# Feed-forward gates and ups by seven half-block products instead of eight, with their result kept in DRAM

## The chip, the cores and the metric

The kernel runs on one core of a Trainium2 chip. The metric is the device time of one execution in microseconds (us), the median over several runs. The engines are named as in the profile: PE is TensorE (PEld its weight load), DVE is VectorE, ACT is ScalarE, POOL is GpSimd, SP is the engine whose queue issues the DMAs.

## What is computed

A trunk of two layers. Each layer normalises the residual stream, puts it through one input projection, three kinds of token mixers and an output projection, and then through a SwiGLU feed-forward; both results are added with a gate. Scale, shift and gate are "modulation" columns, computed from `c` and `c_ctx` by a product with `mod_w`. The change is in the feed-forward (512 latent tokens and, in layer 0 only, 256 context tokens; width 1024; 2816 hidden units):

```python
def swiglu(h, w_in, w_out):
    gate, up = jnp.split(h @ w_in, 2, axis=-1)
    return (jax.nn.silu(gate) * up) @ w_out
...
    for i in range(DEPTH):
        ctx_out = i < DEPTH - 1
        ...
        xl = xl + gt1_l * (jnp.concatenate([ya_l, yb_l, ym_l], axis=-1) @ w_out[i])
        xl = xl + gt2_l * swiglu(modulate(rmsnorm(xl, norm2_g[i]), sh2_l, sc2_l), ffn_w_in[i], ffn_w_out[i])
        if ctx_out:
            xc = xc + gt1_c * (jnp.concatenate([ya_c, yb_c, ym_c], axis=-1) @ w_out[i])
            xc = xc + gt2_c * swiglu(modulate(rmsnorm(xc, norm2_g[i]), sh2_c, sc2_c), ffn_w_in[i], ffn_w_out[i])
```

## The kernel before, in words

Everything is float32. A float32 product is made of three matmuls in the type fp32r: each operand is split into a rounded part (`hi`, a copy by ScalarE, line 227) and the rest (`lo`, a subtraction by VectorE or GpSimd, line 228), and hi x hi, hi x lo and lo x hi are summed in PSUM. `weight` loads 128 output columns of a matrix with a DMA on SP's queue into `wr` and splits them into `wh` and `wl` (two buffers each). `gemm` runs over the 128-row pages of the contraction and makes the three matmuls of each page (line 262) for each span of tokens: 512 columns, and in layer 0 another 256. The result stands in one of five PSUM buffers `gm`.

The last part of a layer goes like this. The mixers' result is split into pages; for each of eight output tiles m of 128 rows `residual` (line 1323) adds the output projection, times its modulation, to X in SBUF. The norm (`norm_stat`, `norm_scale`, `norm_page`) makes the pages `hpage` of the feed-forward's input: a multiply that reads X and a PSUM row of scales (line 364), a scale and shift by ScalarE (line 365), and a split, the odd pages' by GpSimd. The 22 hidden tiles of 128 units are then done in three parts of 8, 7 and 7 (`PARTS`). For each tile of a part the gate and up columns are loaded, multiplied with the eight pages, and joined: ScalarE's tanh (line 1490) and two VectorE rows (lines 1491 and 1492) make silu(gate) x up, which is split into a page `hid` that stays in SBUF. After each part, for each m, the matching rows of the second matrix are multiplied with these pages and added to X.

The modulation columns that later parts of the kernel need are made on VectorE between all this, by `mod_some`: it takes some of a list `todo`, loads a page `wd` of 512 KB and reduces it against `silu(c)` (`mod_dve`, line 320). In layer 0's feed-forward it takes two after each hidden tile and one after each m.

Nothing orders these steps by hand but `issue_after` and `behind`, which keep an instruction behind another: a scheduler puts each engine's instructions in a fixed order when the kernel is built, and pools with a given number of buffers decide how far one step can run ahead of another. Each engine goes through its own list in order, and SP through its DMAs.

Of the kernel before, what the change touches and what calls it, by code (L numbers as in the profile page):

```python
# [11 lines left out]
F32 = mybir.dt.float32  # L12
# [3 lines left out]
ALU = mybir.AluOpType  # L16
# [28 lines left out]
PARTS = (8, 7, 7)  # L45
EPS = 1e-6
# [130 lines left out]
def trunk(ctx, tc, I, out, dbg=None):  # L177
# [194 lines left out]
    xs = dr.tile([P, KD, TL], F32, name="xs")  # L372

# [969 lines left out]

    early = ExitStack()
    xm = early.enter_context(pool("xm"))
    with pool("x0") as xp, pool("p0", 2, space=PSUM) as pm:
# [4 lines left out]
        cb, t = silu_rows(xm, pm)  # L1351
# [26 lines left out]
    marks = (md, mm)  # L1378
    todo = [(0, m) for m in range(16, 48)] + [(1, m) for m in range(48)]

    def mod_some(n, wk, bufs, ins):

        with tc.issue_after(ins.ins):
            for _ in range(min(n, len(todo))):
                mod_dve(*todo.pop(0), cb, t, wk, bufs)

    for l in range(DEPTH):
# [6 lines left out]
        with pool(f"pm{l}", 2, space=PSUM) as pm, pool(f"pc{l}", 1, space=PSUM) as pc, \  # L1394
# [7 lines left out]
            with pool(f"tp{l}") as tp, behind(marks if l == 0 else ()):  # L1402
                data = rwkv_in(l, ctx_out, h, rp, rq, tp, pm, pgm, both, lambda i: mod_some(2 if l == 0 else 0, xm, 4, i))
# [23 lines left out]
        with ExitStack() as st:  # L1427
            xp = st.enter_context(pool(f"x{l + 1}", 1, "right"))
            X = xp.tile([P, KD, T], F32, name="X")
            with behind(loads[3:4]):  # L1430
                xload(X, l)
            tmp = st.enter_context(pool(f"ft{l}", 2, "right"))
            pm = st.enter_context(pool(f"ps{l}", 2, space=PSUM))
            pgm = st.enter_context(pool(f"pf{l}", 5, space=PSUM))
            if l == 0:
                cb, t = silu_rows(tmp, pm)

            yh = pages(KD, KORD)
# [91 lines left out]
```

## Time and profile before

| | |
|---|---|
| median of 3 runs | 2280.55 us (2273.83 to 2282.71) |
| the profiled execution: its time, its span | 2283.55 us, 2281.8 us |
| TensorE busy, granted clock | 95%, .959 |
| VectorE, ScalarE, GpSimd busy | 61%, 37%, 14% |
| share of the chain that ended last | TensorE 81%, VectorE 10%, ScalarE 4% |
| `gm` matmuls of line 262 in that chain | 57% |

The profile is of one execution. Busy shares are averages over the whole span; the chain follows the work that ended last backwards, so it says where each engine set the end. A matmul's time is best read from the distance of its start from the next one's, since matmuls overlap in the pipeline.

### The profile page before, as it was taken

What the parts mean: (1) busy time and instruction counts of PE and PEld (TensorE: products, weight loads), DVE (VectorE), ACT (ScalarE), POOL (GpSimd) and SP (SyncE); (2) the same over time, 40 slices, a digit from 0 to 9 for tenths busy, and PEclk for the clock granted to TensorE, in tenths of its full rate; (3) what the DMA queues carried; (4) which work ended last, traced back from release to release, by engine and by line L of the source; (5) the groups of instructions that cost most, each with busy time, mean ns of one, the idle gap of its engine ahead of it and who ended that gap; (6) DMA issues with size and microseconds to landing.
All of it is one profiled execution on the core that took longest, in us unless ns stands there. A gap on an engine that the chain in (4) does not pass through costs nothing.

```text
span 2281.8 us, 36365 instructions
## 1 busy us (share of the span) xinstructions
PE 2159.2 (95%) x14604; PEld 1780.9 (78%) x14604; DVE 1381.9 (61%) x2706; ACT 844.7 (37%) x1527; POOL 314.2 (14%) x482
## 2 busy tenths in 40 slices
PE   7999997997999999999999999999898998999999
PEld 4788886784668788888888878787685677888887
DVE  6687777895547766554444455788796545334343
ACT  4433333664552421122122354433473544222231
POOL 1022322332201100000000111113142211000000
PEclk9999997897999999999999989999697998999999
DMA  7241112232115334344432312211232122323323
GB/s 289 84 153 52 62 41 74 77 88 56 42 70 155 100 114 146 111 129 135 133 112 83 109 52 63 73 57 39 85 100 59 35 74 83 101 94 94 100 92 102
DMA packets 87352, 211.99 MB, mean 93 GB/s; under 512 B 10248, under 2 KB 33680, under 8 KB 86544
## 3 DMA queue, kind: packets, MB, share of 16 engines
q1 hardware_dynamic: 87184, 209.67, 29.2%
q8 instruction: 115, 1.88, 0.3%
q14 instruction: 53, 0.43, 0.1%
HBM read 187.62 MB, written 22.02 MB: 92 GB/s over the span
## 4 chain that ended last, share of the span: by engine, by line
PE 81%; DVE 10%; ACT 4%; DMA 2%; issue 2%; POOL 1%; SPq 0%; DVEq 0%; ACTq 0%; POOLq 0%
PE gm L262 57%; PE po L1034 4%; PE psm L585 2%; PE inv L660 2%; PE st L1028 1%; DVE cT L320 1%; PE st L1029 1%; PE st L1030 1%; PE mx L1008 1%; PE psm L514 1%; PE pB L700 1%; DVE wl L228 1%; PE psm L573 1%; ACT hu L365 1%; PE up L246 1%
## 5 line engine op out<-in xcount | busy, mean ns | idle before, releaser
L262 PE MATMUL gm<-hpage,wh 128*128 128x512 f32 (+1 forms) x3744 | 1001.7, 355 | 15.3 <-ACT hpage L227 8.9
L262 PEld LDWEIGHTS gm<-hpage,wh 128*128 128x128 f32 x3744 | 664.2, 191 | 119.8 <-ACT hpage L227 11.0
L262 PE MATMUL gm<-hpage,wl 128*128 128x512 f32 (+1 forms) x1872 | 657.4, 353 | 1.9 <-DVE wl L228 1.8
L227 ACT ACTIVATE wh<-wr 128x1024 fp32r<-128x1024 f32 (+2 forms) x214 | 221.6, 1036 | 560.7 <-PE gm L262 457.6
L262 PEld LDWEIGHTS gm<-hpage,wl 128*128 128x128 f32 x1872 | 358.1, 191 | 50.6 <-DVE wl L228 2.5
L228 DVE TENSOR_TENSOR wl<-wr,wh 128x1024 fp32r<-128x1024 f32 (+2 forms) x214 | 258.2, 1207 | 186.9 <-ACT wh L227 185.1
L262 PE MATMUL gm<-hid,wh 128*128 128x512 f32 (+1 forms) x1056 | 282.6, 356 | 0.0
L262 PEld LDWEIGHTS gm<-hid,wh 128*128 128x128 f32 x1056 | 185.6, 188 | 32.2
L262 PE MATMUL gm<-hid,wl 128*128 128x512 f32 (+1 forms) x528 | 187.4, 356 | 0.0
L1323 DVE SCALAR_TENSOR_TENSOR X<-gm,mod,X 128x512 f32<-128x512 f32 (+1 forms) x100 | 64.0, 643 | 191.0 <-PE gm L262 187.7
L320 DVE CUSTOM_DVE_ANT_0 cT<-wd,cB,mod_b 128x1024 f32<-128x1024 f32 x140 | 177.7, 1300 | 1.1 <-DMA wd<-in_mod_d 0.7
L1492 DVE SCALAR_TENSOR_TENSOR ft<-ft,gm 128x512 f32<-128x512 f32 x66 | 39.5, 598 | 153.0 <-PE gm L262 152.7
L1010 DVE TENSOR_REDUCE mr<-mx 128x1 fp32r<-128x768 f32 (+1 forms) x80 | 67.9, 848 | 83.8 <-PE mx L1008 83.6
L1034 PE MATMUL po<-pe,hpage 128*128 128x512 f32 (+1 forms) x224 | 112.2, 590 | 0.5 <-ACT pe L1032 0.4
L262 PEld LDWEIGHTS gm<-hid,wl 128*128 128x128 f32 x528 | 99.0, 188 | 16.1
L338 POOL TENSOR_TENSOR acc<-acc,sq 128x512 f32<-128x512 f32 (+1 forms) x15 | 23.9, 1601 | 604.0 <-ACT sq L337 604.0
L1032 ACT ACTIVATE pe<-st 128x512 f32<-128x512 f32 (+1 forms) x112 | 62.9, 563 | 89.8 <-PE st L1030 88.7
L227 ACT ACTIVATE hid<-ft 128x512 fp32r<-128x512 f32 x66 | 36.2, 549 | 128.4 <-DVE ft L1492 128.4
L1028 PE MATMUL st<-k,k 97*128 97x512 f32 (+1 forms) x112 | 78.0, 698 | 4.7 <-ACT k L1015 4.1
L1490 ACT ACTIVATE ft<-gm 128x512 f32<-128x512 f32 x66 | 33.9, 514 | 90.4 <-PE gm L262 90.3
L1008 PE MATMUL mx<-k,k 96*128 96x256 f32 (+1 forms) x144 | 46.3, 396 | 17.1 <-DVE mr L1010 9.9
L585 PE MATMUL psm<-pr,kb 64*128 64x128 f32 (+1 forms) x384 | 57.7, 308 | 1.4 <-POOL pr L555 1.4
(425 smaller groups left out, 3128.5 us busy)
## 6 DMA issues: line engine op xcount, KB each, us to landing
wr<-in_ffn_in SPq DMA_DIRECT2D x88, 512.0 KB, 3.5
wd<-in_mod_d SPq DMA_DIRECT2D x86, 512.0 KB, 3.8
wr<-in_w_in SPq DMA_DIRECT2D x44, 512.0 KB, 3.6
wr<-in_ffn_out SPq DMA_DIRECT2D x34, 448.0 KB, 3.4
wr<-in_w_out SPq DMA_DIRECT2D x20, 512.0 KB, 3.7
wr<-in_ffn_out SPq DMA_DIRECT2D x16, 512.0 KB, 3.6
zs<-ze SPq DMA_DIRECT2D x26, 256.0 KB, 2.0
X<-in_xT SPq DMA_DIRECT2D x16, 384.0 KB, 6.4
```

Source lines behind the costliest of these rows:

```text
L227: ac.activation(hi, src, AF.Copy)
L228: return en.tensor_tensor(lo, src, hi.bitcast(F32), ALU.subtract)
L262: pe.matmul(ps, x[:, j], act[k][y][:, a:b], start=(i == 0 and n == 0), stop=(i == len(kl) - 1 and n == 2))
L320: ve.tensor_tensor_reduce(out=t[:, s], in0=w, in1=cb[:, s], scale=1.0, scalar=modb[:, l, m:m + 1], op0=ALU.mult, op1=ALU.add, accum_out=mo ...
L585: pe.matmul(pa[j][:, p, c], flat(kb[hr, d, p, c]), flat(pr[hr, d, p, c, 0:nq]), start=True, stop=True)
L660: i = pe.matmul(v8(o)[hr, q], a[hr, d, p, c], b[hr, d, p, c], start=True, stop=True)
L1008: pe.matmul(ps[:, a - k0:b - k0], qh[0:96, n * P:(n + 1) * P], kh[0:96, a:b], start=True, stop=True)
L1010: ve.tensor_reduce(mr[:, n - q0:n - q0 + 1], ps[:, :T - k0], AX.X, ALU.max)
L1028: pe.matmul(ps, kh[0:97, ks], qh[0:97, qs], start=True, stop=False)
L1032: ac.activation(e, ps, AF.Exp, scale=QK_SCALE)
L1034: pe.matmul(po[:, :w], v, e, start=(kt == kts[0]), stop=(kt == kts[-1]))
L1323: return ve.scalar_tensor_tensor(X[:, m, a:b], ps, mods[l][:, 24 * which + 16 + m, s:s + 1], X[:, m, a:b], ALU.mult, ALU.add)
```

## The change

A pair of gate and up columns of one hidden tile, 256 output columns in all, against 1024 rows and all tokens, is seen as a 2 by 2 block product: the blocks of the weights are gate and up by upper and lower four pages, those of the activations are upper and lower four pages by first and second half of the tokens. Of the 22 tiles of each layer the first two (`PLAIN`) are done as before; for the other 20 the eight block products are replaced by seven products of sums of blocks (Strassen's scheme in Winograd's form).

- The sums of activation blocks are made once for each layer (`halves`: eight subtractions by VectorE, eight by GpSimd, twelve splits, and four more splits before the first such tile). For that the norm keeps its unsplit output in `ru`, all eight pages.
- The sums of weight blocks are made for each tile: four additions of 128x512 by GpSimd (`wsum`, lines 1472 to 1475 of the new kernel) and five splits of 128x512 (`ws`), beside the split of the gate columns.
- The seven products of a tile have 4 pages x 3 matmuls each on half of the tokens (`product`); seven additions on VectorE, each reading one PSUM buffer, and ScalarE's copy of the first product put them together, then the tanh and three VectorE rows make `hid`.
- All 22 tiles are now done before the second matrix. `hid` (unsplit) is written to DRAM (`hd`) and fetched page by page (`fetch`), then split again (`resplit`). X is also written to DRAM (`xm`) and loaded again for the second matrix.
- The modulation reduces move: in layer 0 none stands among the gates; 2 after each m of the output projection as before, and about 72 reduces in the second matrix's three parts (`mod_some(1)` ahead and 1, 3, 2 behind each m); a last part of them in layer 1. `silu_rows`, 16 small transposes, is made anew for the second matrix of each layer.

```diff
+    def halves(l, nt, ru, h, tq):
+
+        n = nt // 2
+        r = []
+        for k in range(4):
+            b11, b12, b21, b22 = ru[:, k, :n], ru[:, k, n:nt], ru[:, k + 4, :n], ru[:, k + 4, n:nt]
...
+            ve.tensor_tensor(b11, b12, b11, ALU.subtract)
+            gp.tensor_tensor(t3, b22, b12, ALU.subtract)
+            ve.tensor_tensor(b22, b22, b11, ALU.subtract)
+            gp.tensor_tensor(b21, b21, b22, ALU.subtract)
+            for t, src in ((t1, b11), (t2, b22), (t4, b21)):
+                split(t[:, 0], t[:, 1], src)
...
+            if j < PLAIN:
...
+            else:
+                if j == PLAIN:
+                    for k in range(4):
+                        b12 = tuple(x[:, n:nt] for x in h[k])
+                        split(*b12, ts[k][2])
...
+                    B = {1: half(0, lo), 2: half(4, lo), 3: half(4, up), 4: tt(3), 5: tt(0), 6: tt(1), 7: half(0, up)}
+                gh, gl, g = weight(I["ffn_in"][l, j, 0], KD, P, raw=True)
+                u = ws.tile([P, KD, P], F32, name="wu", bufs=2)
+                sp.dma_start(out=u, in_=I["ffn_in"][l, j, 1])
+                s1, s2, s3, s4 = (ws.tile([P, 4, P], F32, name="wsum", bufs=3) for _ in range(4))
+                gp.tensor_tensor(s1, u[:, 0:4], u[:, 4:8], ALU.add)
+                gp.tensor_tensor(s2, s1, g[:, 0:4], ALU.subtract)
+                gp.tensor_tensor(s3, g[:, 0:4], u[:, 0:4], ALU.subtract)
+                gp.tensor_tensor(s4, g[:, 4:8], s2, ALU.subtract)
+                A = {1: (gh[:, 0:4], gl[:, 0:4]), 2: (gh[:, 4:8], gl[:, 4:8])}
+                for i, src in ((6, s2), (7, s3), (5, s1), (4, u[:, 4:8]), (3, s4)):
+                    t = ws.tile([P, 2, 4, P], F32R, name="ws", bufs=7)
+                    split(t[:, 0], t[:, 1], src)
+                    A[i] = (t[:, 0], t[:, 1])
+
+                def product(i):
+                    ps = pgm.tile([P, 512], F32, name="gm")[:, :n]
+                    for k in range(4):
+                        for x, y in ((0, 0), (0, 1), (1, 0)):
+                            pe.matmul(ps, A[i][x][:, k], B[i][k][y], start=(k == 0 and x + y == 0),
+                                      stop=(k == 3 and x == 1))
+                    return ps
...
+                ac.activation(c1, product(1), AF.Copy)
+                ve.tensor_tensor(c2, c1, product(6), ALU.add)
+                ve.tensor_tensor(c1, c1, product(2), ALU.add)
+                ac.activation(t1, c1, AF.Tanh, scale=0.5)
+                ve.scalar_tensor_tensor(t1, t1, 1.0, c1, ALU.add, ALU.mult)
+                ve.tensor_tensor(c3, c2, product(7), ALU.add)
+                p5 = product(5)
+                ve.tensor_tensor(ups[:, n:nt], c3, p5, ALU.add)
+                ve.tensor_tensor(c2, c2, p5, ALU.add)
+                ve.tensor_tensor(ups[:, 0:n], c3, product(4), ALU.add)
+                ve.tensor_tensor(g2, c2, product(3), ALU.add)
+                ac.activation(t2, g2, AF.Tanh, scale=0.5)
+                ve.scalar_tensor_tensor(t2, t2, 1.0, g2, ALU.add, ALU.mult)
+                ve.scalar_tensor_tensor(hid[:, :nt], hid[:, :nt], 0.5, ups[:, :nt], ALU.mult, ALU.mult)
+            sp.dma_start(out=hd[l][j, :, :nt], in_=hid[:, :nt])
...
+            def before(m):
+                if part == 0:
+                    mod_some(1)
+
+            def done(m, ins):
+                more(1)
...
+                elif l == 0:
+                    mod_some((1, 3, 2)[part], ins)
...
+    def fetch(l, j, nt, pool, name):
+
+        t = pool.tile([P, 2, T], F32R, name=name)
+        sp.dma_start(out=t[:, 1, :nt].bitcast(F32), in_=hd[l][j, :, :nt])
+        resplit(t[:, :, :nt])
+        return t[:, 0], t[:, 1]
```

The order of the instructions on three places, before and after. Line numbers move a little: the split's subtraction is line 228 before and 229 after, the norm's multiply 364 and 365.

VectorE among the gates of layer 1, before: one hidden tile with its two weight splits (`wl`) and its silu (numbers tell tiles of one name apart).

```order
L228 TENSOR_TENSOR wl_18470<-wr_18468,wh_18469 128x1024
L1491 SCALAR_TENSOR_TENSOR ft_18462<-ft_18462,gm_18412 128x512
L1492 SCALAR_TENSOR_TENSOR ft_18462<-ft_18462,gm_18437 128x512
L228 TENSOR_TENSOR wl_18476<-wr_18474,wh_18475 128x1024
L228 TENSOR_TENSOR hid_18411<-ft_18462,hid_18411 128x512
```

VectorE at the same place after: one of the 20 tiles. `c` and `ups` with a `gm` among their inputs are the additions that read a product in PSUM; `ws` and `wl` are splits, of this tile's weights and of those of tiles to come; `hid` the silu.

```order
L229 TENSOR_TENSOR wl_20696<-wr_20694,wh_20695 128x1024
L1498 TENSOR_TENSOR c3_20443<-c2_20442,gm_20490 128x256
L1497 SCALAR_TENSOR_TENSOR hid_20409<-hid_20409,c1_20441 128x256
L229 TENSOR_TENSOR ws_20577<-wu_20558,ws_20577 128x512
L1500 TENSOR_TENSOR ups_20445<-c3_20443,gm_20504 128x256
L1501 TENSOR_TENSOR c2_20442<-c2_20442,gm_20504 128x256
L229 TENSOR_TENSOR ws_20580<-wsum_20563,ws_20580 128x512
L1502 TENSOR_TENSOR ups_20445<-c3_20443,gm_20519 128x256
L229 TENSOR_TENSOR ws_20710<-wsum_20703,ws_20710 128x512
L1503 TENSOR_TENSOR c4_20444<-c2_20442,gm_20533 128x256
L1505 SCALAR_TENSOR_TENSOR hid_20409<-hid_20409,c4_20444 128x256
L1506 SCALAR_TENSOR_TENSOR hid_20409<-hid_20409,ups_20445 128x512
```

A tile has nine rows whose inputs both lie in SBUF (`ws`, `wl`, `hid`), and seven that read PSUM stand between them, never more than two in a row.

GpSimd at the start of layer 1's feed-forward and to its end, before: the mixers' last rows, the norm's sums and page splits.

```order
L765 TENSOR_TENSOR ph<-vt,bs 128x2x2x64
L995 MEMSET k_17660 1x768
L994 TENSOR_TENSOR k_17661<-kq,k_17660 96x768
L338 TENSOR_TENSOR acc<-acc,sq 128x512 x3
L228 TENSOR_TENSOR hpage<-hu,hpage 128x256 x8
```

GpSimd there after: the last of `halves`, then the weight sums.

```order
L1399 TENSOR_TENSOR ru<-ru 128x256 x3
L1472 TENSOR_TENSOR wsum<-wu 128x512
L1473 TENSOR_TENSOR wsum<-wsum,wr 128x512
L1474 TENSOR_TENSOR wsum<-wr,wu 128x512
L1475 TENSOR_TENSOR wsum<-wr,wsum 128x512
```

Before, GpSimd has no row among the gates; now four for each of the 20 tiles follow each other to the end of its list, and nothing else stands between.

VectorE in the norm of layer 0 between output projection and feed-forward, before: `hu` is a page times its scale, `hpage` a page's split.

```order
L364 TENSOR_TENSOR hu<-X,psm 128x512 x3
L228 TENSOR_TENSOR wl<-wr,wh 128x1024
L338 TENSOR_TENSOR acc<-acc,sq 128x256
L228 TENSOR_TENSOR hpage<-hu,hpage 128x512
L364 TENSOR_TENSOR hu<-X,psm 128x512
L228 TENSOR_TENSOR hpage<-hu,hpage 128x512
```

VectorE there after: the product now goes to `ru`.

```order
L1326 SCALAR_TENSOR_TENSOR X<-gm,mod_85,X 128x256
L365 TENSOR_TENSOR ru<-X,psm 128x512 x8
L339 TENSOR_TENSOR acc<-acc,sq 128x256
L229 TENSOR_TENSOR wl<-wr,wh 128x1024
L229 TENSOR_TENSOR hpage<-ru,hpage 128x512 x2
L350 TENSOR_SCALAR ms<-ss 128x2
```

Before, three pages are multiplied ahead of the first split, and the other five between splits; now all eight come first.

## Rows read from the trace of the kernel before

**Rows 1.** Part 1 of the page: busy time and share of the span.

```profile
PE 2159.2 (95%) x14604; PEld 1780.9 (78%) x14604; DVE 1381.9 (61%) x2706; ACT 844.7 (37%) x1527; POOL 314.2 (14%) x482
```

**Rows 2.** The chain, in order of time: start, length, engine, line, count (us).

```profile
771.38 530.00 PE gm L262 x3027
...
1912.23 365.77 PE gm L262 x1584
```

**Rows 3.** Stretches: length, busy us and count of PE, PEld, DVE, ACT, POOL; clock, DMA.

```profile
772.00:1302.00 530.00, 530.00 (x3034) 465.78 (x3033) 272.19 (x407) 112.64 (x164) 7.88 (x6) 1.00 0.38 120
794.07:810.75 16.68, 16.68 (x99) 14.77 (x98) 10.34 (x17) 3.93 (x6) 0.00 (x0) 1.00 0.39 127
887.75:954.84 67.09, 67.09 (x386) 58.29 (x384) 40.93 (x61) 8.79 (x9) 0.00 (x0) 1.00 0.44 142
2162.42:2238.39 75.97, 75.97 (x336) 62.87 (x335) 29.68 (x34) 21.22 (x27) 0.00 (x0) 1.00 0.31 95
```

**Rows 4.** A stretch of 256-column matmuls of layer 0: length, busy, count, clock, DMA.

```profile
799.08:804.83 5.75, 5.75 (x48) 1.00 0.00 0
```

**Rows 5.** TensorE in order of time, first and last of 20 matmuls.

```profile
477.15 0.33 PE L248 MATMUL up<-wh,hpage 128*128 128x384 f32 x1
...
480.44 0.34 PE L247 MATMUL up<-wl,hpage 128*128 128x384 f32 x1
```

**Rows 6.** Groups by form: busy us, mean ns, idle before.

```profile
L228 DVE TENSOR_TENSOR wl<-wr,wh 128x1024 fp32r<-128x1024 f32 x172 | 213.6, 1242 | 173.8 <-ACT wh L227 172.5
L320 DVE CUSTOM_DVE_ANT_0 cT<-wd,cB,mod_b 128x1024 f32<-128x1024 f32 x140 | 177.7, 1300 | 1.1 <-DMA wd<-in_mod_d 0.7
L1323 DVE SCALAR_TENSOR_TENSOR X<-gm,mod,X 128x512 f32<-128x512 f32 x60 | 45.0, 750 | 148.7 <-PE gm L262 145.4 <-issue 3.3
L228 DVE TENSOR_TENSOR wl<-wr,wh 128x896 fp32r<-128x896 f32 x34 | 37.1, 1091 | 12.8 <-ACT wh L227 12.5
L227 ACT ACTIVATE wh<-wr 128x1024 fp32r<-128x1024 f32 x172 | 182.4, 1061 | 438.4 <-PE gm L262 348.2 <-issue 75.5 <-DMA wr<-in_w_in 7.1
```

**Rows 7.** VectorE in order of time, norm of layer 0: start, length, line, count.

```profile
744.36 1.88 DVE L364 TENSOR_TENSOR hu<-X,psm 128x512 f32<-128x512 f32 x3 [0.41 <-PE psm L356]
...
747.63 0.68 DVE L228 TENSOR_TENSOR hpage<-hu,hpage 128x512 fp32r<-128x512 f32 x1
...
748.96 1.29 DVE L228 TENSOR_TENSOR hpage<-hu,hpage 128x512 fp32r<-128x512 f32 x1
...
750.28 1.28 DVE L364 TENSOR_TENSOR hu<-X,psm 128x512 f32<-128x512 f32 x2
...
753.90 1.25 DVE L222 SCALAR_TENSOR_TENSOR nwtn<-nwtn,ms 128x2 f32<-128x2 f32 x1
...
759.00 1.08 DVE L364 TENSOR_TENSOR hu<-X,psm 128x256 f32<-128x256 f32 x3 [2.58 <-PE psm L356]
```

**Rows 8.** GpSimd in order of time, the same stretch.

```profile
748.42 1.27 POOL L228 TENSOR_TENSOR hpage<-hu,hpage 128x512 fp32r<-128x512 f32 x1 [34.71 <-ACT hpage L227]
750.62 1.28 POOL L228 TENSOR_TENSOR hpage<-hu,hpage 128x512 fp32r<-128x512 f32 x1 [0.92 <-ACT hpage L227]
753.64 1.49 POOL L228 TENSOR_TENSOR hpage<-hu,hpage 128x512 fp32r<-128x512 f32 x1 [1.74 <-ACT hpage L227]
```

**Rows 9.** TensorE in order of time: transposes of `silu_rows`, then the norm.

```profile
668.59 1.09 PE L311 MATMUL psm<-c_id,sc 128*128 128x128 f32 x8
...
747.18 0.93 PE L262 MATMUL gm<-hpage,wh 128*128 128x512 f32 x2 [2.85 <-ACT hpage L227]
...
749.70 0.63 PE L262 MATMUL gm<-hpage,wh 128*128 128x512 f32 x1
750.13 0.63 PE L262 MATMUL gm<-hpage,wl 128*128 128x512 f32 x1
```

**Rows 10.** DMA issues: operation, count, KB each, median us to landing.

```profile
wd<-in_mod_d SPq DMA_DIRECT2D x86, 512.0 KB, 3.8
...
lz<-zs SPq DMA_DIRECT2D x8, 384.0 KB, 3.4
```

More of the change, by code (lines that the diff above doesn't have):

```diff
@@ L45 @@
 PARTS = (8, 7, 7)
+PLAIN = 2
 EPS = 1e-6
@@ L228, in split, with weight @@
         return en.tensor_tensor(lo, src, hi.bitcast(F32), ALU.subtract)
-    def weight(src, k, m, en=ve):
-        raw = wp.tile([P, 1024], F32, name="wr", bufs=2)[:, :k * m].rearrange("p (k m) -> p k m", m=m)
+    def weight(src, k, m, en=ve, raw=False):
+        r = wp.tile([P, 1024], F32, name="wr", bufs=2)[:, :k * m].rearrange("p (k m) -> p k m", m=m)
         hi = wp.tile([P, 1024], F32R, name="wh", bufs=2)[:, :k * m].rearrange("p (k m) -> p k m", m=m)
         lo = wp.tile([P, 1024], F32R, name="wl", bufs=2)[:, :k * m].rearrange("p (k m) -> p k m", m=m)
-        sp.dma_start(out=raw, in_=src)
-        split(hi, lo, raw, en)
-        return hi, lo
+        sp.dma_start(out=r, in_=src)
+        split(hi, lo, r, en)
+        return (hi, lo, r) if raw else (hi, lo)
     def pages(n, order=None):
@@ L372, in trunk @@
     xs = dr.tile([P, KD, TL], F32, name="xs")
+    xm = [dr.tile([P, KD, T], F32, name=f"xm{l}") for l in range(DEPTH)]
+    hd = [dr.tile([KF, P, T], F32, name=f"hd{l}") for l in range(DEPTH)]
     def in_weight(l, m):
@@ L1342, in behind, with residuals, add @@
         return st
+    def residuals(l, nt, X, tmp, pm, pgm):
+        def add(which, get, act, order, before, each, after=None, raw=None):
+            if after is not None:
+                rng = spans(nt) if nt > TL else ((0, 256), (256, 512))
+                acc = tmp.tile([P, T], F32, name="acc", bufs=1)
+                last = KD - 4
+            else:
+                last = KD
+            for m in range(last):
+                before(m)
+                for ps, a, b in gemm(pgm, get(m), act, spans(nt), order):
+                    i = residual(l, which, X, m, ps, a, b)
+                    if after is not None:
+                        norm_stat(acc, X, m, a, b, tmp, gp)
+                each(m, i)
+            if after is None:
+                return
+            gain(*after)
+            hn, tail = None, [(m, None) for m in range(last, KD)]
+            for a, b in rng:
+                held = []
+                for m, w in tail:
+                    w = w or get(m)
+                    held.insert(0, (m, w if m >= KD - 2 else None))
+                    for ps, _, _ in gemm(pgm, w, act, ((a, b),), order):
+                        residual(l, which, X, m, ps, a, b)
+                        norm_stat(acc, X, m, a, b, tmp, ve)
+                tail = held
+                if hn is None:
+                    hn = pages(KD)
+                bc = norm_scale(acc, ((a, b),), pm)[0][0][0]
+                for k in range(KD):
+                    norm_page(*after, X, hn, bc, k, a, b, tmp, raw)
+            return hn
+        return add
@@ L1350, in trunk @@
         xload(X, 0)
-        cb, t = silu_rows(xm, pm)
+        cb, t = silu_rows(xm0, pm)
         for k in range(KD):
@@ L1516 @@
+        h = ffn(l, ctx_out, nt, y, mstack, loads, marks)
 def kernel(**inputs):
```

188 lines of the change are left out of this document (100 added, 88 removed).

## Prediction

> **What bounds the kernel now.** I read the busy shares first: TensorE is busy 95% of the span, VectorE 61% [rows 1]. The chain of work that ended last then says whether that share is the limit where the change acts: the feed-forward of layer 0 is a single link of 530.00 us of `gm` matmuls, that of layer 1 one of 365.77 us [rows 2]. Inside those links nothing but TensorE sets the end, so a matmul taken out there is worth its full pitch until another engine takes over. The table of stretches tells how near the others are [rows 3]: in the first, the 530 us, VectorE works 272.19 us and GpSimd (POOL) 7.88; in a gate stretch of layer 1, 29.68 and nothing of 75.97. GpSimd is as good as idle there, and the change puts work on it.
>
> **What is taken out on TensorE.** A tile of 128 hidden units has 48 matmuls of 512 columns, in layer 0 also 48 of 256. One such tile in layer 0 takes 16.68 us (the second of the stretches); seven of layer 1, the last, take 75.97, so 10.85 each [rows 3]. Twenty tiles per layer now have 84 matmuls of half the tokens: 384 columns in layer 0, 256 in layer 1. 48 matmuls of 256 columns took 5.75 us, .1198 each [rows 4]. Twenty of 384 columns start 3.29 us apart over 19 steps, .1732 each [rows 5]; that is another stage's line, but the same form and gap-free. So a tile needs 14.55 us in layer 0 (-2.13) and 10.06 us in layer 1 (-.79). If TensorE stays the limit: -42.6 and -15.8 us.
>
> **What VectorE and GpSimd get.** Per tile VectorE has the 1024-wide `wl` and five 512-wide splits of weight sums, seven adds that read a product from PSUM, and three products of SBUF tiles. Rows that follow each other overlap a little: three of 512 columns took 1.88 us in all, where one alone takes .68, so a pitch of .60; three of 256 took 1.08, so .33 [rows 7]. `wl` is 1.24 less the same .08, 1.15 [rows 6]; between these, 768 columns .87 and 384 .47. Layer 1: 1.15 + 5 x .60 + 7 x .33 + 2 x .33 + .60 = 7.7 us a tile. Layer 0: 1.15 + 3.0 + 7 x .47 + 2 x .47 + .87 = 9.25. Both fit beside TensorE's 10.06 and 14.55. GpSimd gets four additions 128x512; the two-input row of that shape there takes 1.27 to 1.28 us [rows 8], so 5.0 a tile with the overlap of a row on the next. That fits too, if the two engines can work side by side.
>
> The trace says that they can't always. VectorE's split of a page started at 748.96 and took 1.29 us, where the same row alone takes .68: it ended .56 after the GpSimd row of 748.42 to 749.69. A step on two columns at 753.90 took 1.25 and ended when the GpSimd row of 753.64 ended. But two `hu` rows from 750.28, which read PSUM and one SBUF tile, took 1.28 together, their normal pitch, under the GpSimd row of 750.62 [rows 7, 8]. So a VectorE row with two SBUF inputs and a GpSimd row with two exclude each other for the whole row; one that reads PSUM goes on. The Trainium skill, "SBUF — State Buffer", section "Who interferes with whom", states this as an exclusive lock for the whole instruction between a VectorE instruction with two SBUF inputs and a GpSimd one that reads SBUF, and that order of issue decides who blocks; the rows agree, and the rule speaks against this change. Taken at its hardest (no PSUM row ever falls under a GpSimd row) it makes a layer 1 tile 12.7 us, taken away 10.06.
>
> From the rows: of layer 1's 7.7 us a tile, 5.4 are two-input rows (nine of them), 2.3 are the seven PSUM reads. The lock alone needs 5.4 + 5.0 = 10.4, already above 10.06. VectorE issues in order, so under a GpSimd row it can only finish the PSUM reads that come next, until the next two-input row stands still. In the new order nine two-input rows and seven PSUM reads alternate: after a two-input row come on average 7/9 of a read, .26 us. Each of the four GpSimd rows thus costs VectorE 1.25 - .26 = .99, and the tile becomes 7.7 + 4 x .99 = 11.7 us, bound by VectorE and GpSimd together: **+.85 us a tile, +17 us** instead of -15.8. Bounds: each GpSimd row over one full read (.33) gives 11.4 (+11); none 12.7 (+37). In layer 0 the full sum is 9.25 + 5.0 = 14.25, under 14.55, so there TensorE keeps the lead and **-42.6 us** stands. ScalarE (one 1024-wide copy of 1.06 us [rows 6], five of half that width, three smaller: under 6 us) is hidden.
>
> **What stands around the tiles.**
> - Two more `silu_rows`: 32 small transposes at about .12 us (eight in 1.09 [rows 9]): +4.
> - The norm of layer 0: VectorE now makes all eight multiplies of a block before the first split, where three stood. TensorE already waits 2.85 us there for the first page, then runs at half clock (.43 us pitch at 512 columns) [rows 9]; five more at .60 are +3, and the lock about +1: +4 (0 to 7).
> - The sums of activation halves in layer 0: on VectorE 8 + 12 + 4 rows of 384 (11.3), four `wl` (4.6), the two plain tiles' products (3.7), two refetches (1.7); on GpSimd eight (about 8): 29.3 of 33.4 us that the two plain tiles cover. Hidden on paper, but pieces wait for each other: +3 (0 to 8).
> - The same in layer 1: 24 x .33 + 4.6 + 2.4 + 1.2 and the first tile's splits 4.1, together 20.2 on VectorE, 10.9 on GpSimd, against 21.7 us of plain tiles: +3 (0 to 9).
> - `hid` through DRAM: the fifth to eighth page can be fetched when product 7 has released the `h` pages; a 384 KB load takes 3.4 us to land [rows 10], its copy and subtraction 1.8: 5.2 us against 36 matmuls, 6.2 in layer 0 and 4.3 in layer 1, and the first pages' matmuls: +2 (0 to 6). The reload of X (eight loads) stands behind it; five PSUM buffers hold its residuals for two and a half output tiles. Cover gone, it would cost up to 6.
> - The output phase of layer 0 has 72 modulation reduces that lay under gates before. A part of eight pages takes 67.09/8 = 8.39 us per output tile (the third stretch), one of seven 7.34 [rows 3]. VectorE there, in the second part: `wl` 1.01, a residual of 512 columns .67 and one of 256 .4, four reduces at 1.28 with their accumulator step: 7.2 [rows 6]; with seven refetches of .87 in the first two or three tiles, 10. TensorE then waits for `wl`: +4 (0 to 16; a `wd` load needs 3.8 us to land [rows 10], behind three buffers).
>
> Together +20 (8 to 35).
>
> **The sum**, on the profiled execution's 2283.55 us (3.0 above the median of the runs, 2280.55): 2283.55 - 42.6 + 17 + 20 = 2278, 5.6 less; on the median that is **2275 us**.
>
> **Rivals.**
> - *The lock costs nothing in layer 1* (GpSimd's rows fall under PSUM reads and waits, TensorE stays the bound): 10.06 a tile, 2280.55 - 42.6 - 15.8 + 20 = 2242. For it: GpSimd can run ahead by its buffers. Against: 10.4 us of locked rows a tile cannot be packed into 10.06, so only shorter rows than those shown would do it. I keep .20 for that and for an order in which I have misread who waits.
> - *The lock at its hardest* (the slower side): VectorE's adds wait for their product, and GpSimd's rows fall between two-input rows. 12.7 us a tile: +37 in layer 1, 2280.55 - 42.6 + 37 + 20 = 2295; with GpSimd rows of 1.49 us as the one at 753.64 [rows 8] layer 0 comes to 9.25 + 6 = 15.2 (+14 more) and layer 1 to 13.7: 2329 at the worst, about 2305 between. It is slower by more than .5% from a layer 1 tile of 12.55 us on: (11.4 + 42.6 - 20)/20 = 1.7 above 10.85. The Trainium skill's rule on order of issue ("SBUF — State Buffer", same section) leaves open which of the two it is.
> - *The refetch and the moved reduces bind the output phase of layer 0*: +16 instead of +4, and norm and first tiles at their upper ends: 2275 + 12 + 15 = 2302.
> - *Gaps lower the clock*: in layer 1 TensorE would work 10.06 of 11.7 us. After the one gap of 2.85 us the pitch was .43 instead of .23 for some 6 us [rows 9]. Gaps here would be under 2 us each; at half clock for half of the 20 tiles it is +100.
>
> **Chances.** Forecast as computed, 2260 to 2295: .56. Lock without cost, 2230 to 2258: .20. Hardest lock or output phase: .20, 2293 to 2310. Clock: .04. A measurement of this kernel can tell about .5%, 11.4 us. Faster than 2269: .20 and a quarter of the first, .34; slower than 2292: .24 and a tenth of the first, .30; same .36. Range 2240 to 2303.
>
> **What would show it.** Right: tiles of layer 0 at 14.5 to 14.6 us with TensorE gap-free; tiles of layer 1 at 11.4 to 12, TensorE waiting for `ws` and `wl` of VectorE; VectorE's 512-wide subtractions longer than .69 and GpSimd's sums longer than 1.28 there, the PSUM adds unchanged. Wrong: layer 1 tiles at 10.1, or layer 0 tiles above 14.8; gaps of tens of us at the boundaries; a granted clock below 1 in the 20 tiles of layer 1.

## The result and the profile after

The changed kernel takes 2293.38 us (median of 5 runs, 2290.14 to 2295.45) against 2280.55 us before (5 runs, 2273.83 to 2282.75): a ratio of 1.0053, interval 1.0031 to 1.0076. It is a little slower; the forecast was a little faster, 2275 us. The profiled execution of after took 2290.14 us, the lowest of its runs, with a span of 2288.4; that of before, 2283.55, is above all of the five. So the spans of the two profiles are only 6.6 us apart, where the medians are 12.8 apart. What follows is worked out between the two profiles; the other 6.2 us lie between executions, and no trace locates them.

The page of after: busy time and share of each engine, and, below, the chain that ended last by engine.

```profile
PE 2122.9 (93%) x15116; PEld 1811.0 (79%) x15116; DVE 1707.6 (75%) x3172; ACT 951.5 (42%) x1765; POOL 572.9 (25%) x658
...
PE 63%; DVE 21%; issue 6%; DMA 5%; ACT 4%; POOL 0%; SPq 0%; DVEq 0%; ACTq 0%; POOLq 0%
```

GpSimd's busy time has grown from 14% of the span to 25%, VectorE's from 61% to 75% [rows 1]. The chain was 81% TensorE and 10% VectorE; now VectorE has 21%. In which layer that is, the stretches tell. I cut each trace at the norms, from the first matmul of a norm's statistics to the next norm's: layer 0's norm and feed-forward, what lies between, and layer 1's to the end. First before, then after (columns: start and end, length, then busy us and count of PE, PEld, DVE, ACT, POOL, granted clock, DMA share, GB/s).

```profile
736.16:1301.32 565.16, 560.69 (x3204) 492.01 (x3203) 298.60 (x464) 136.71 (x206) 16.17 (x14) 0.99 0.37 117
1301.32:1893.50 592.18, 554.59 (x4460) 443.13 (x4458) 396.75 (x887) 273.38 (x528) 123.89 (x210) 0.93 0.22 66
1893.50:2281.80 388.30, 374.84 (x1650) 307.30 (x1648) 157.71 (x209) 109.23 (x149) 6.06 (x8) 0.98 0.31 95
```

```profile
738.51:1278.71 540.20, 525.65 (x2980) 494.02 (x2979) 448.65 (x650) 190.88 (x304) 150.71 (x108) 0.98 0.50 157
1278.71:1869.51 590.80, 548.90 (x4459) 438.42 (x4458) 395.31 (x887) 274.67 (x528) 121.11 (x204) 0.94 0.22 68
1869.51:2288.40 418.89, 374.71 (x2386) 335.66 (x2384) 336.69 (x489) 160.27 (x289) 135.01 (x96) 0.97 0.42 134
```

Layer 0 became 25.0 us shorter, layer 1 30.6 us longer, and the rest (2281.8 and 2288.4 less these two) 1.0 longer: +6.6. Now the 20 changed tiles alone, from the first to the last of their matmuls, in layer 0 and layer 1 of after.

```profile
801.65:1097.39 295.74, 293.60 (x1681) 292.96 (x1680) 239.66 (x327) 112.21 (x183) 117.13 (x76) 1.00 0.36 108
1919.43:2159.98 240.55, 214.43 (x1681) 206.04 (x1679) 231.36 (x324) 97.11 (x182) 116.72 (x77) 0.99 0.37 114
```

In layer 0 they took 295.74 us, where 20 tiles of before are 333.6 (16.68 each [rows 3]): -37.9, 14.79 us a tile. In layer 1 they took 240.55, where 20 tiles of before are 217.0 (10.85 each): +23.5, 12.03 us a tile. TensorE is busy 293.60 of 295.74 in the first, 214.43 of 240.55 in the second: there it waits, while VectorE is busy 231.36. In the chain, the layer 0 stretch still has one long link of TensorE (start, length, line, count):

```profile
852.39 245.34 PE gm L1486 x1404
```

It is 1404 matmuls in 245.34 us, .1747 each. Layer 1's link of 365.77 us [rows 2] is gone: between 1940 and 2175 us the chain goes through 474 short pieces, and the lines with the largest shares among them are issue and VectorE's `ws` splits.

What happens in a layer 1 tile is seen when VectorE and GpSimd are laid side by side. First VectorE in order of time (start, length, line), one period of 12.15 us from 2073.87 to 2086.02; then GpSimd's four weight sums; then TensorE's waits.

```profile
2073.87 0.68 DVE L229 TENSOR_TENSOR ws<-wsum,ws 128x512 fp32r<-128x512 f32 x1
2074.48 0.41 DVE L1494 TENSOR_TENSOR c<-c,gm 128x256 f32<-128x256 f32 x1
2074.81 1.66 DVE L229 TENSOR_TENSOR ws<-wsum,ws 128x512 fp32r<-128x512 f32 x1
2076.39 0.41 DVE L1495 TENSOR_TENSOR c<-c,gm 128x256 f32<-128x256 f32 x1
2076.72 2.20 DVE L229 TENSOR_TENSOR wl<-wr,wh 128x1024 fp32r<-128x1024 f32 x1
2078.85 0.41 DVE L1498 TENSOR_TENSOR c<-c,gm 128x256 f32<-128x256 f32 x1
2079.18 1.17 DVE L1497 SCALAR_TENSOR_TENSOR hid<-hid,c 128x256 f32<-128x256 f32 x1
2080.27 0.68 DVE L229 TENSOR_TENSOR ws<-wu,ws 128x512 fp32r<-128x512 f32 x1
...
2082.47 1.67 DVE L229 TENSOR_TENSOR ws<-wsum,ws 128x512 fp32r<-128x512 f32 x1
...
2084.95 0.43 DVE L1505 SCALAR_TENSOR_TENSOR hid<-hid,c 128x256 f32<-128x256 f32 x1 [0.48 <-ACT hid L1504]
2085.42 0.69 DVE L1506 SCALAR_TENSOR_TENSOR hid<-hid,ups 128x512 f32<-128x512 f32 x1
2086.02 0.69 DVE L229 TENSOR_TENSOR ws<-wsum,ws 128x512 fp32r<-128x512 f32 x1
```

```profile
2074.64 1.28 POOL L1475 TENSOR_TENSOR wsum<-wr,wsum 128x512 f32<-128x512 f32 x1 [3.20 <-DVE ws L229]
2076.55 1.29 POOL L1472 TENSOR_TENSOR wsum<-wu 128x512 f32<-128x512 f32 x1 [0.63 <-DVE ws L229]
2077.92 2.15 POOL L1473 TENSOR_TENSOR wsum<-wsum,wr 128x512 f32<-128x512 f32 x1
2082.30 1.30 POOL L1474 TENSOR_TENSOR wsum<-wr,wu 128x512 f32<-128x512 f32 x1 [2.23 <-DVE ws L229]
```

```profile
2079.31 1.70 PE L1486 MATMUL gm<-t,ws 128*128 128x256 f32 x12 [0.76 <-DVE c L1498]
...
2081.67 0.50 PE L1486 MATMUL gm<-hpage,wh 128*128 128x256 f32 x2 [0.66 <-DVE c L1501]
```

Rows with a `gm` among their inputs (products in PSUM) take their .41 us also beside a GpSimd row, as those of 2074.48 and 2078.85 beside the GpSimd rows of 2074.64 and 2077.92. The split at 2074.81 takes 1.66 instead of .68, for it ends .55 after GpSimd's row of 2074.64 to 2075.92. The `wl` of 2076.72 takes 2.20 instead of 1.22 for the same reason, and while it then runs, GpSimd's next row, begun at 2077.92, stands still in turn (2.15 instead of 1.28); at 2079.18 VectorE's `hid` waits for that one (1.17 instead of .43). The two engines take turns row by row. Over the tile VectorE stands still .98 + .98 + .74 + .99 = 3.7 us for GpSimd's four rows, and .48 for ScalarE's tanh (2084.95). TensorE's waits name VectorE's additions: they come late, PSUM buffers stay taken, and TensorE stops .76 and .66 us in this tile.

### The profile page after: what moved, and what is told of

The parts are those of the page before. It is cut to its first block, busy times and chain, and to the rows that moved or that the text cites. A ratio compares the mean times of both kernels' runs of the same rounds, so it can differ in the third digit from the quotient of the medians.

```text
span 2288.4 us, 38958 instructions
## 1 busy us (share of the span) xinstructions
PE 2122.9 (93%) x15116; PEld 1811.0 (79%) x15116; DVE 1707.6 (75%) x3172; ACT 951.5 (42%) x1765; POOL 572.9 (25%) x658
## 4 chain that ended last, share of the span: by engine, by line
PE 63%; DVE 21%; issue 6%; DMA 5%; ACT 4%; POOL 0%; SPq 0%; DVEq 0%; ACTq 0%; POOLq 0%
PE gm L263 28%; PE gm L1486 12%; PE po L1037 4%; DVE ws L229 3%; PE psm L588 2%; DVE cT L321 2%; DVE wl L229 2%; PE inv L663 2%; PE st L1031 1%; DMA wd<-in_mod_d 1%; PE st L1032 1%; DMA hq<-hd 1%; PE st L1033 1%; PE mx L1011 1%; DVE hpage L229 1%
## 5 line engine op out<-in xcount | busy, mean ns | idle before, releaser
L263 PE MATMUL gm<-hpage,wh 128*128 128x512 f32 (+1 forms) x2352 | 636.3, 356 | 24.2 <-ACT hpage L228 8.2
L263 PEld LDWEIGHTS gm<-hpage,wh 128*128 128x128 f32 x2352 | 418.1, 193 | 94.4 <-ACT hpage L228 13.8
L263 PE MATMUL gm<-hpage,wl 128*128 128x512 f32 (+1 forms) x1176 | 414.6, 354 | 2.0 <-DVE wl L229 1.8
L1486 PE MATMUL gm<-t,ws 128*128 128x384 f32 (+1 forms) x1440 | 226.8, 310 | 11.6 <-DVE c L1498 11.5
L1486 PEld LDWEIGHTS gm<-t,ws 128*128 128x128 f32 x1440 | 214.2, 189 | 15.0 <-DVE c L1498 14.5
L229 DVE TENSOR_TENSOR ws<-wsum,ws 128x512 fp32r<-128x512 f32 x160 | 154.0, 965 | 10.0 <-ACT ws L228 9.5
L1486 PE MATMUL gm<-hpage,wh 128*128 128x384 f32 (+1 forms) x640 | 144.9, 315 | 15.2 <-DVE c L1501 15.2
L1486 PE MATMUL gm<-hpage,ws 128*128 128x384 f32 (+1 forms) x960 | 156.2, 311 | 1.5 <-DVE ups L1502 1.4
L1486 PEld LDWEIGHTS gm<-hpage,ws 128*128 128x128 f32 x960 | 146.0, 189 | 2.0 <-issue 1.6
L263 PE MATMUL gm<-hq,wh 128*128 128x512 f32 (+1 forms) x528 | 142.6, 357 | 0.0
L1486 PEld LDWEIGHTS gm<-hpage,wh 128*128 128x128 f32 x640 | 107.6, 190 | 20.4 <-DVE c L1501 19.0
```

What stands on the lines that cost most here:

```text
L229: return en.tensor_tensor(lo, src, hi.bitcast(F32), ALU.subtract)
L263: pe.matmul(ps, x[:, j], act[k][y][:, a:b], start=(i == 0 and n == 0), stop=(i == len(kl) - 1 and n == 2))
L1486: pe.matmul(ps, A[i][x][:, k], B[i][k][y], start=(k == 0 and x + y == 0), stop=(k == 3 and x == 1))
```

## The experiments

The theory is that of the prediction (its "lock"), sharpened: VectorE's rows with two SBUF inputs and GpSimd's two-input rows take turns, and in layer 1 this makes VectorE's list longer than TensorE's. The main rival: the tile is long because VectorE's own list with its waits for products and for ScalarE is long, or because sums come late, whatever GpSimd does. A second: the tiles are not what loses, but the passage through DRAM and the moved reduces. Ratios are to runs of the kernel before made beside each experiment (their medians 2281.41 to 2282.86 us).

**The sums on VectorE.** The four additions of a tile change the engine.

```diff
-                gp.tensor_tensor(s1, u[:, 0:4], u[:, 4:8], ALU.add)
+                ve.tensor_tensor(s1, u[:, 0:4], u[:, 4:8], ALU.add)
...
```

> The four weight sums of a tile are made by VectorE instead of GpSimd. Theory (VectorE and GpSimd exclude each other for whole rows, and that sets layer 1's tiles): each sum costs VectorE .60 us instead of about .92 us of standing still, so a layer 1 tile falls from 12.03 us to 10.3 to 10.7 (7.7 + 2.4, and up to .5 of wait for ScalarE's tanh) and one of layer 0 from 14.79 to 14.6; together 30 to 38 us faster than the changed kernel, 2253 to 2263. Rival (the tile is VectorE's own list with its waits for products and for ScalarE, whatever GpSimd does): a tile of layer 1 grows by 4 x .60 to 14.4, 45 us slower, about 2338.

Measured: 2255.12 us, ratio to the kernel before .9871 (.9843 to .9899). Its two stretches of 20 tiles:

```profile
806.25:1099.30 293.05, 293.05 (x1681) 293.05 (x1680) 248.20 (x401) 113.96 (x184) 0.00 (x0) 1.00 0.35 108
1922.56:2129.89 207.33, 204.47 (x1681) 201.35 (x1680) 202.62 (x396) 99.63 (x181) 0.00 (x0) 1.00 0.42 132
```

10.37 us a tile in layer 1, 14.65 in layer 0. VectorE has four rows more per tile and is busy less in layer 1 (202.62 instead of 231.36 us): what was taken away is standing still. Of the 33.2 us that layer 1's tiles gained, 28.7 are busy time of VectorE and the rest is waiting: in the changed kernel VectorE waited 7.8 us in these tiles for ScalarE's tanh (the view is shown with the two sums below), and here it doesn't, since the scheduler has put other rows between the addition and the row that needs the tanh. The rival's 14.4 us a tile is refuted.

**No sums at all.** The splits take quarters of the weights as they were loaded.

```diff
-                s1, s2, s3, s4 = (ws.tile([P, 4, P], F32, name="wsum", bufs=3) for _ in range(4))
-                gp.tensor_tensor(s1, u[:, 0:4], u[:, 4:8], ALU.add)
...
+                s1, s2, s3, s4 = u[:, 0:4], g[:, 0:4], g[:, 4:8], u[:, 4:8]
```

> Leaves out the four weight sums of each tile: the splits take quarters of the weights as loaded, so the products are of other data. GpSimd has no row among the tiles. Theory (lock): VectorE's ws row of 512 columns goes back to .68 us and wl to 1.24, a layer 1 tile is bound by TensorE, 10.06 to 10.2 us (-37 in 20 tiles), one of layer 0 14.55 to 14.6 (-4): 2250 in all. Rival (VectorE's own list and its waits): layer 1 stays at 11.5 to 12.0, nothing in layer 0, 2285.

Measured: 2246.36 us (one run).

```profile
797.02:1090.08 293.06, 293.06 (x1682) 293.06 (x1680) 202.05 (x320) 111.25 (x179) 0.00 (x0) 1.00 0.33 107
1915.26:2115.92 200.66, 200.66 (x1680) 200.65 (x1679) 168.86 (x326) 103.89 (x185) 0.00 (x0) 1.00 0.46 139
```

10.03 and 14.65 us a tile, TensorE busy without a gap in both. That is the pace of the matmuls, and it shows that ScalarE's tanh, the seven PSUM additions and the DMAs are no limit at this pace. 14.65, not 14.55, is what 84 matmuls of 384 columns take here.

**Layer 1 as before the change, and both layers.** `plain` tiles go on to the last one, and no halves are made.

```diff
+        plain = PLAIN if l == 0 else KF
...
-            if j < PLAIN:
+            if j < plain:
```

> Layer 1 makes all 22 tiles as before the change, without sums of activation halves; layer 0 is as changed. Theory (layer 1's tiles are what loses): 20 x (12.03 - 10.85) = 24 us and some 4 us of layer 1's halves come back: 2262 to 2268, faster than the kernel before by about .7%. Rival (the loss in layer 1 is the passage through DRAM and the norm's new order, not the tiles): at most 8 us come back, 2285.

Measured: 2270.3 us, ratio .9948 (.9932 to .9965). Layer 0's and layer 1's stretch:

```profile
741.14:1281.90 540.76, 525.79 (x2980) 494.11 (x2979) 448.97 (x650) 190.68 (x304) 150.93 (x108) 0.98 0.48 157
...
1877.03:2274.90 397.87, 377.90 (x1666) 310.51 (x1664) 169.07 (x225) 111.08 (x153) 8.03 (x8) 0.97 0.43 136
```

Layer 1 is 397.87 us instead of 418.89: 21.0 come back, with layer 0 as changed; the time is 2 us above the range that was expected. So layer 1's tiles are what loses. Not all of it, though: before, the stretch was 388.30.

> Both layers make all 22 tiles as before the change, without halves; what is left of the change is the norm's new order, the passage of the product and of X through DRAM, the second transposes and the moved reduces. By the terms of the prediction these are 4 + 4 + 2 + 4 and a little in layer 1's norm: 14 to 18 us slower than the kernel before, 2294 to 2300. If the passage through DRAM is hidden and the moved reduces too: 2283 to 2288. If it is what loses: above 2305.

Measured: 2299.27 us, ratio 1.0068 (1.0047 to 1.0089), as the sum of the terms had it.

```profile
737.86:1307.74 569.88, 561.13 (x3220) 493.65 (x3219) 288.40 (x426) 135.01 (x188) 19.05 (x20) 0.99 0.45 146
...
1899.47:2297.60 398.13, 378.29 (x1666) 310.83 (x1664) 169.41 (x225) 111.29 (x153) 8.13 (x8) 0.97 0.43 136
```

By stretch the sum was not right: layer 0 has lost only 4.7 us by the norm's new order, the passage through DRAM and the 72 moved reduces, and layer 1 9.8. In layer 1 of this kernel and of the one above, the scheduler has put the last eight reduces not into the second matrix but into the norm, where VectorE waits for their `wd` loads while the first gates' `wl` stands behind them; VectorE, and TensorE's wait:

```profile
1935.63 1.28 DVE L321 CUSTOM_DVE_ANT_0 cT<-wd,cB,mod_b 128x1024 f32<-128x1024 f32 x1 [1.56 <-DMA wd<-in_mod_d]
...
1938.75 1.22 DVE L229 TENSOR_TENSOR wl<-wr,wh 128x1024 fp32r<-128x1024 f32 x1
```

```profile
1940.02 0.80 PE L263 MATMUL gm<-hpage,wl 128*128 128x512 f32 x1 [4.36 <-DVE wl L229]
```

In the changed kernel itself these reduces stand in layer 1's second matrix, and its layer 1 loses only 7.1 us outside the 20 tiles (30.6 less 23.5).

**GpSimd rows that nobody waits for.** The sums are on VectorE; GpSimd makes four like them whose result isn't read.

```diff
+                d = ws.tile([P, 4, P], F32, name="dm", bufs=1)
+                for _ in range(4):
+                    gp.tensor_tensor(d, u[:, 0:4], u[:, 4:8], ALU.add)
```

> The weight sums are made by VectorE as in e1_sums_on_vector, and GpSimd makes four additions 128x512 per tile whose result nobody reads. It tells the lock from the delay of a chain of sums that comes late. Theory (VectorE's rows with two SBUF inputs stand still while a GpSimd row reads): each of the four rows costs VectorE .9 to 1.0 us again, a layer 1 tile goes from 10.4 to 14.0 to 14.4, one of layer 0 from 14.65 to 15.0 to 15.6: 80 to 95 us slower than e1, 2335 to 2350. Rival (in the changed kernel the products waited for sums that GpSimd finished late): nobody waits for these, so 2255 as e1.

Measured: 2353.64 us (one run), 98.5 more than without these rows and a little above the expected range.

```profile
801.87:1125.16 323.29, 300.52 (x1680) 293.45 (x1681) 315.29 (x403) 106.69 (x186) 118.80 (x73) 0.99 0.31 99
1950.39:2224.28 273.89, 231.12 (x1680) 225.35 (x1679) 271.25 (x402) 103.59 (x185) 115.76 (x75) 0.90 0.31 101
```

13.69 us a tile in layer 1 (+3.33, .83 for each unread row), and 16.16 in layer 0 (+1.51), where VectorE's list is now too long as well. The granted clock in layer 1's stretch fell to .90, but VectorE is busy 271.25 of its 273.89 us, so VectorE sets the pace. By form, VectorE's rows in layer 1 (count, busy us, mean ns):

```profile
L229 DVE TENSOR_TENSOR ws<-wsum,ws 128x512 fp32r<-128x512 f32 x76 | 71.1, 954 | 0.0
...
L1508 DVE SCALAR_TENSOR_TENSOR hid<-hid,c 128x256 f32<-128x256 f32 x18 | 20.5, 1142 | 0.0
...
L1498 DVE TENSOR_TENSOR c<-c,gm 128x256 f32<-128x256 f32 x20 | 8.2, 408 | 0.0
```

The two-input rows are longer on average (954 and 1142 ns), the additions that read PSUM are not (408). Nobody reads what GpSimd makes here, and no wait of any engine or queue in the two stretches names it, so a late chain of sums is ruled out; only the turns are left.

**GpSimd rows that only write.**

```diff
+                d = ws.tile([P, 4, P], F32, name="dm", bufs=1)
+                for _ in range(10):
+                    gp.memset(d, 0.0)
+                ac.activation(ws.tile([P, 1], F32, name="dn"), d[:, 0, 0:1], AF.Copy)
```

> As e1_sums_on_vector, and GpSimd writes a constant ten times per tile into a tile of 128x512 of which one column is read (ten rows of .52 us, as long as the four sums). Theory (what excludes is the GpSimd row's reading from SBUF): nothing, 10.4 us per layer 1 tile and 2253 to 2260. Rival (any long GpSimd row on SBUF stops VectorE's two-input rows): as the unread sums, 13.5 to 14.5 us per tile, 2330 to 2350.

Measured: 2263.87 us (one run), 4 above the theory's range and far below the rival's.

```profile
800.13:1095.27 295.14, 295.14 (x1682) 295.14 (x1680) 248.57 (x402) 116.46 (x203) 97.24 (x185) 1.00 0.34 108
1917.27:2133.21 215.94, 201.91 (x1680) 198.17 (x1679) 204.16 (x397) 102.27 (x201) 95.03 (x181) 0.99 0.39 128
```

```profile
L229 DVE TENSOR_TENSOR ws<-wsum,ws 128x512 fp32r<-128x512 f32 x52 | 34.5, 683 | 0.2 <-ACT ws L228 0.2
...
L229 DVE TENSOR_TENSOR wl<-wr,wh 128x1024 fp32r<-128x1024 f32 x13 | 15.9, 1225 | 7.0 <-ACT wh L228 6.9
```

GpSimd is busy 95.03 us in layer 1's stretch, and VectorE's two-input rows are as if it weren't (683 and 1225 ns). The .43 us a tile over the first experiment are ScalarE's: its row that reads the constant waits for the memsets, and `wh` stands behind it, as VectorE's idle time before `wl` names.

**Two of four sums.** The first and the third sum go to VectorE.

```diff
-                gp.tensor_tensor(s1, u[:, 0:4], u[:, 4:8], ALU.add)
+                ve.tensor_tensor(s1, u[:, 0:4], u[:, 4:8], ALU.add)
...
-                gp.tensor_tensor(s3, g[:, 0:4], u[:, 0:4], ALU.subtract)
+                ve.tensor_tensor(s3, g[:, 0:4], u[:, 0:4], ALU.subtract)
```

> Two of the four weight sums (the first and the third) go to VectorE, two stay on GpSimd. Theory (a price for each GpSimd row): VectorE's list is 7.7 + 2 x .60 + 2 x .92 us of standing still and .4 of wait for ScalarE, 11.1 to 11.3 us per layer 1 tile, half way between the changed kernel's 12.03 and 10.37 with all four on VectorE; layer 0 at TensorE's 14.65: 2270 to 2276. Rival (a chain that runs through both engines, so that a tile pays for each hand-over): 11.8 us or more, 2283.

Measured: 2266.64 us (one run), below both ranges.

```profile
1920.23:2137.38 217.15, 204.72 (x1680) 201.47 (x1679) 214.32 (x365) 99.83 (x186) 60.03 (x38) 1.00 0.42 129
```

10.86 us a tile, 1.2 less than with four rows on GpSimd and .5 more than with none. Two rows on GpSimd cost .24 us each more than on VectorE, the other two .6 each. I had added .4 us of wait for ScalarE, and without it the sum is 7.7 + 2 x .60 + 2 x .92 = 10.74: the wait did not show. VectorE's waits for the tanh in the 20 tiles of layer 1 (us in total, times, longest), first in the changed kernel, then here:

```profile
DVE hid L1505 <- ACT hid L1504: 7.8, 16, 0.5
...
DVE hid L1505 <- ACT hid L1504: 0.5, 1, 0.5
```

In the changed kernel's list the row that needs the tanh (line 1505) stands right behind the addition that ScalarE reads (line 1503); here, as in the first experiment, other rows stand between. So the wait belongs to the order of the list, and some .37 of the 1.2 us a tile are this wait, not GpSimd's rows. A price for each hand-over, the rival's 11.8, is refuted.

**What is left to gain.** From the first experiment on, also the eight subtractions of activation halves go from GpSimd to VectorE.

```diff
-            gp.tensor_tensor(t3, b22, b12, ALU.subtract)
+            ve.tensor_tensor(t3, b22, b12, ALU.subtract)
...
-            gp.tensor_tensor(b21, b21, b22, ALU.subtract)
+            ve.tensor_tensor(b21, b21, b22, ALU.subtract)
```

> As e1_sums_on_vector, and the eight subtractions of activation halves that GpSimd made go to VectorE too. Theory: each costs VectorE .33 to .47 us instead of about .55 of standing still, so the stretch before the first product of layers 0 and 1 gets 1 to 2 us shorter each: 2251 to 2254. Rival (VectorE is the engine that this stretch waits for, and more rows make it longer): 2258 to 2262.

Measured: 2241.33 us, ratio .9817 (.9792 to .9842).

```profile
739.98:1270.30 530.32, 520.86 (x2981) 491.62 (x2980) 457.51 (x738) 191.58 (x304) 17.84 (x20) 0.99 0.49 160
1270.30:1856.86 586.56, 544.47 (x4459) 435.22 (x4458) 396.19 (x887) 273.64 (x528) 124.87 (x204) 0.94 0.23 68
1856.86:2241.10 384.24, 364.04 (x2386) 331.23 (x2384) 310.44 (x577) 163.37 (x289) 6.07 (x8) 0.98 0.45 146
```

The time is 10 us below the expected range. Layer 0 is 5.6 us shorter than in the first experiment (530.32 against 535.90), more than the 1 to 2 that I expected; layer 1 .7. Another 5.7 came from the stretch between (586.56 against 592.31) and 4.4 from what lies ahead of layer 0's norm (739.98 against 744.39); no edit touches either. So I ran it again.

> The kernel of e8_halves_on_vector once more, in five rounds: the stretch between the two feed-forwards, which no edit touches, was 586.6 us there and 592.3 in e1. If that is the order that the scheduler gave, it is 586 to 588 again and the time 2238 to 2243; if it is the run, it is nearer 592 and the time 2244 to 2248.

Measured: 2239.93 us, ratio .9819 (.9804 to .9833), the stretch between 587.6 us. Layer 0 took 533.0 us this time, so of its 5.6 us only about 3 came again; the stretch ahead of layer 0's norm ends anywhere from 735 to 744 us in the profiles of these experiments. The gain in the stretch between belongs to the order that the scheduler gave to this program, in which rows of the mixers have moved too; why it is better I did not find out.

With four plain tiles at the head of each layer, and with one:

```diff
-PLAIN = 2
+PLAIN = 4
```

```diff
-PLAIN = 2
+PLAIN = 1
```

> As e8_halves_on_vector, with four plain tiles at the head of each layer instead of two. Costs 2 x (16.68 - 14.65) = 4.1 us in layer 0 and 2 x (10.85 - 10.4) = .9 in layer 1. Theory (some 7 us are lost in layer 0 because the halves aren't ready when the plain tiles end): 5 to 7 come back, -1 in all, 2250 to 2254. Rival (what is lost there lies in the norm, ahead of the plain tiles): 5 us slower, 2257 to 2259.

> As e8_halves_on_vector with one plain tile at the head of each layer instead of two. Gain of one more tile 2.0 us in layer 0 and .4 in layer 1. Theory (two plain tiles, 33 us, just cover the sums of halves and the first tile's splits, and one doesn't): 5 to 12 us slower, 2246 to 2253. Rival (the sums were late only because of GpSimd's rows): 2239.

Measured: 2248.87 us for four, ratio .9857 (.9832 to .9882), and 2263.41 us for one, ratio .9918 (.9899 to .9938). Both miss their ranges: that for four was set against 2255 us, before the 2241 with two plain tiles were known, and one is 10 us above its own. Four cost 7.5 us more than two: layer 0 became 3.6 to 6.2 us longer, where 4.1 of cost were expected, so nothing comes back there, and the stretch between is back at 591.3. One costs 22 to 23.5 more than two: 12 to 15 lie in layer 0, and again some 6 in the stretch between (593.1). With one, TensorE stands before the second product (first row: the wait in brackets), and its clock falls (second row: 20 us of that place, the granted clock .57):

```profile
793.59 1.01 PE L1486 MATMUL gm<-t,ws 128*128 128x384 f32 x2 [9.84 <-ACT ws L228]
```

```profile
780.00:800.00 20.00, 8.93 (x31) 8.42 (x32) 16.02 (x28) 6.18 (x13) 0.00 (x0) 0.57 0.40 138
```

Two plain tiles just cover the halves and the first splits.

## Why the prediction was wrong

The reading of the profile was right, the sign of the sum was not: the cost in layer 1's tiles was put 6.5 us too low and the gain in layer 0's 4.7 too high. With the 1.0 elsewhere these make the 12.2 us between the forecast for the profiled execution (5.6 less) and its 6.6 more.

- **Layer 1's tiles, the step that failed by its size.** The prediction took 11.7 us, +17; measured were 12.03, +23.5. The lock itself it had right: 4 x .99 = 3.96 us of standing still, measured 3.7. VectorE is busy 231.36 us in the 20 tiles, 11.57 a tile, where 11.7 were forecast. What the prediction put at nothing is time in which VectorE stands idle: .46 us a tile, .39 of it the wait for ScalarE's tanh between two of its rows (7.8 us in 16 of the tiles). In the tile shown, .14 more go where a row needs the result of the row just before it (`hid` of 2084.95, the next one .47 behind it instead of .33). I had called ScalarE hidden because it has time to spare; but its answer stands in the middle of VectorE's list. No experiment was made for this wait alone; it is gone where the order of the list has other rows in that place (the first experiment and the two sums).
- **Layer 0's tiles.** 14.55 us forecast, -42.6; measured 14.79, -37.9. The 384-column pitch is .1744 to .1747, not .1732 (2 us in 20 tiles), and the first 276 matmuls took 50.4 us instead of 48.2. There TensorE stopped twice, .87 us at 836.20 and 1.27 at 852.39, because VectorE had stood still 2.66 and 2.45 us for a refetched page of `hid` (`hq`), whose DMA ScalarE's copy waited for. The first of the two, VectorE and then TensorE:

```profile
834.26 0.96 DVE L1409 TENSOR_TENSOR hq<-hq 128x768 fp32r<-128x768 f32 x1 [2.66 <-ACT hq L1408]
...
836.20 0.62 PE L1486 MATMUL gm<-hpage,wh 128*128 128x384 f32 x2 [0.87 <-DVE c L1501]
```

  The prediction had counted two refetches as busy time (1.7 us, in the plain tiles) and no wait for one. With the sums on VectorE TensorE has no such stop, and all 20 tiles go at 14.65.
- **What stands around the tiles** was +20 in the forecast and is +12.9 in layer 0 (-25.0 less -37.9) and +7.1 in layer 1: +20.0. By layers the forecast had 14 and 6 (the transposes and the passage through DRAM halved between them). That the sum came out is in part luck: in layer 0 the terms other than the sums of halves were put at 11 and are 4.7 in the kernel with plain tiles only, and what then falls to the halves and first splits, 8.2, was put at 3.
- **The rivals.** "The lock costs nothing" is refuted: 10.03 us a tile is reached only in the kernel without sums, and unread sums on GpSimd alone make a tile of 10.37 one of 13.69. "The lock at its hardest" had 12.7 us a tile and 2295 us, near the measured 2293, but not its mechanism: PSUM rows do run under GpSimd's rows. The refetch and the reduces did not bind layer 0 (+4.7 with everything but the new tiles, and the 2.1 us of the two stops above), and the granted clock stayed at 1.00 and .99 in the two stretches of tiles.
- **What it should have weighed.** The Trainium skill, "Perfetto Trace Analysis", section "Optimizing Scalar/DVE Operations", says that GpSimd and VectorE share a read port, so moving work from one to the other might not help. The runs agree and go further: here moving it back helps, by 33 us in layer 1's tiles (240.55 to 207.33), some 8 of them by the order that did away with the wait for the tanh. The prediction worked out both prices, .99 for a row on GpSimd and .60 for the same row on VectorE, and did not set them side by side. The Trainium skill, "SBUF — State Buffer", section "Who interferes with whom", says "for the whole instruction", which the prediction draws on, of VectorE's 2-port modes; of rows with two SBUF inputs it says that they contend with GpSimd rows that read. That such rows exclude each other row by row is what the rows here show.

## What to carry to other kernels

Work that is given to an idle GpSimd beside a busy VectorE is paid for on VectorE, if both read two SBUF inputs: here .74 to .99 us for a 128x512 row that VectorE itself makes in .60. A saving on TensorE is worth its pitch only down to the next engine's list, and that list holds its waits for short answers of other engines too, not only its busy rows, unless the order puts other rows in their place. With the sums and the halves on VectorE the same idea is 1.8% faster than the kernel before instead of .5% slower; some 5 us of that, .2%, lie in the stretch between the feed-forwards, which the change does not touch.

## What I had not expected of the hardware

VectorE and GpSimd take turns row by row: a GpSimd row that has begun stands still in its turn, 2.15 us instead of 1.28 at 2077.92, when VectorE's `wl` goes first. Rows of GpSimd that only write (.53 us for 128x512) leave VectorE's two-input rows at 683 ns; the Trainium skill, "SBUF — State Buffer", section "Who interferes with whom", says the same of rows that only write, and the run agrees.
